# A pool of their own for the norms' small tiles, and a gap that puts large tiles at multiples of 512 bytes

## The chip, the cores and the metric

The kernel runs on one core of a Trainium2 chip. The metric is the time of one execution on the device in microseconds (us). Five engines work side by side: TensorE (PE in the rows; its weight loads are PEld), VectorE (DVE), ScalarE (ACT), GpSimd (POOL) and SyncE (SP), which issues the DMAs.

## The reference, cut to what matters

Two transformer blocks over 256 tokens of width 1024, all in float32. Nearly all of the arithmetic is in matrix products of the normed tokens with large weights:

```python
def first_block(x, p, ...):
    h = rmsnorm(x, norm_mix_g)
    u_rwkv, u_attn, u_gate = split(h @ w_in)
    o_a, o_b = rwkv7_time_mix(u_rwkv, ...), diff_attention(u_attn, ...)
    x = x + (sig(g_a) * (o_a @ w_proj_a) + sig(g_b) * (o_b @ w_proj_b)) @ w_out
    x = x + square(relu(rmsnorm(x, norm_mlp_g) @ w_ff1)) @ w_ff2          # 1024 -> 4096 -> 1024
    x = x + (p @ w_ple) * sigmoid(rmsnorm(x, norm_ple_g) @ w_ple_gate)
    return rmsnorm(x, final_norm_g)

def second_block(x, ...):
    for layer in range(2):
        x = x + 0.5 * swiglu(rms_norm(x, norm_ffn1[layer]), gate, up, down)   # 1024 -> 2816 -> 1024
        x = x + mix(rms_norm(x, norm_mix[layer]) @ w_in, ...) @ w_out[layer]  # attention
        x = x + 0.5 * swiglu(rms_norm(x, norm_ffn2[layer]), gate, up, down)
    return x
```

## The kernel before, in words

**Products.** A float32 product is made of three float32r products: each operand is split into a rounded high part and the rest, and `mm3` (which calls `mm`, the matmul of L279, three times) adds high x high, high x low and low x high in one PSUM bank. The stationary operand of a matmul is a 128x128 block of the tokens (transposed), the moving operand a 128x512 block of a weight; a chunk of 256 weight columns, and the attention's values, make 128x256 moving blocks, and the first block's queries and keys 128x384. In the rows `b<-hi,hTh` is such a matmul: bank, moving tile, stationary tile.

**Weights.** `wunit` brings 128x1024 floats (512 KB) into one of 3 `raw` buffers by a DMA on SyncE, `split` makes `hi` on ScalarE (L365) and `lo` on VectorE (L366). There are 5 buffers of each, and 6 more after the first stage.

**Tokens.** `Normed` (one for each 128 tokens) multiplies by the gain, flips by four PE transposes at a time (L283) and splits into `hTh` and `hTl`; its sum of squares `ss` and what `rstd` and `rsqrt` make of it are tiles of one to two floats a row. In `mlp` the gate's and up's products use hTh and hTl as stationary; the activation `a` is flipped into `aTh` and `aTl`, which are stationary for `down`. The first stage has `hT1h` and `hT1l` instead of hTh and hTl.

**Order.** The order of PE's instructions is written out by hand (`Weave` decides where side work is put between the large products); the other engines' order comes from the program's. Neither looks at addresses.

**Where tiles lie.** Each pool takes a stretch of the rows of SBUF in the order in which the pools are opened, and in a pool the tags follow each other in the order of first use; a tile takes its row's bytes, rounded up to 32. So a small tile shifts all that lie behind it. In the program as built the rows begin, in bytes and modulo 512:

| tile | pool | begins at | modulo 512 |
|---|---|---|---|
| x, h | xp, act | 17536, 25728 | 128 |
| ss, ms, rsi_x, rsh_x, rsa_x (two of each) | act | 42112 to 42431 | - |
| hTh, hTl (two of each) | act | 42432 to 58815 | 448 |
| sy, msg, r2 and the other small tiles of the last norm | act | 58816 to 59455 | - |
| raw | raw | 59456 | 64 |
| hi, lo (all eleven of each) | hl, hlx | 71744 | 64 |
| hT1h, hT1l | mix | 112704 | 64 |
| aTh, aTl of four of the five `mlp`s | mlp, ph0, ph2, ph5 | e.g. 172096 | 64 |
| aTh, aTl of the `mlp` before the second attention (ph3) | ph3 | e.g. 179296 | 96 |

In the last row the tile `fbias` (8 floats) lies ahead: the constants of the second attention are brought during that mlp, and shift it by 32 bytes. A column block of a tile begins a multiple of 512 bytes behind the tile, so it has the tile's residue. The only exception are blocks of the 264 columns of one attention weight (48 matmuls).

Of the kernel before, what the change touches and what calls it, by code (L numbers as in the profile page):

```python
# [7 lines left out]
F32 = mybir.dt.float32  # L8
# [100 lines left out]
class Mark:  # L109


    def __init__(self):
        self.done, self.at, self.res = False, 0.0, None
# [105 lines left out]
class Ker:  # L219


    def __init__(self, ctx, tc, d):
        self.tc, self.nc, self.d = tc, tc.nc, d
        nc = self.nc
        ctx.enter_context(tc.manual_schedule(engines={mybir.EngineType.PE}))
        self.W = Weave()
        self.const = ctx.enter_context(tc.tile_pool(name="const", bufs=1))
        self.xp = ctx.enter_context(tc.tile_pool(name="xp", bufs=1))
        self.act = ctx.enter_context(tc.tile_pool(name="act", bufs=2))
        self.ps = ctx.enter_context(tc.tile_pool(name="ps", bufs=1, space=PSUM))  # L230
        self.banks = Slots(self.W, self.ps, "b", [128, 512], 8)
        self.quota, self.held = 2, 0
        self.x = [self.xp.tile([128, D], F32, name=f"x{t}") for t in range(2)]
        self.pre = None

    def make_ident(self):
        nc = self.nc
        self.ident = self.const.tile([128, 128], F32, name="ident")
        nc.sync.dma_start(out=self.ident, in_=self.cst("ident"))
        self.identb = self.bf_const(self.const, "identb")  # L240
# [139 lines left out]
    def rsqrt(self, pool, m, n, tag):  # L380

        nc = self.nc
        i = pool.tile([128, n], I32, name=f"rsi_{tag}", tag=f"rsi_{tag}")
        mh = pool.tile([128, n], F32, name=f"rsh_{tag}", tag=f"rsh_{tag}")
        a = pool.tile([128, n], F32, name=f"rsa_{tag}", tag=f"rsa_{tag}")
        nc.vector.tensor_scalar(out=i, in0=m.bitcast(I32), scalar1=1, scalar2=None, op0=ALU.arith_shift_right)
        nc.vector.tensor_scalar(out=mh, in0=m, scalar1=-0.5, scalar2=None, op0=ALU.mult)
        nc.vector.tensor_scalar(out=i, in0=i, scalar1=-1.0, scalar2=float(0x5F3759DF), op0=ALU.mult, op1=ALU.add)
        y = i.bitcast(F32)
        for _ in range(3):  # L390
            if n == 1:
                nc.vector.scalar_tensor_tensor(out=a, in0=y, scalar=mh, in1=y, op0=ALU.mult, op1=ALU.mult)
            else:
                nc.vector.tensor_tensor(out=a, in0=y, in1=y, op=ALU.mult)
                nc.vector.tensor_tensor(out=a, in0=a, in1=mh, op=ALU.mult)
            nc.vector.scalar_tensor_tensor(out=y, in0=a, scalar=1.5, in1=y, op0=ALU.add, op1=ALU.mult)
        return y
# [15 lines left out]
        self.nc.scalar.activation(out=self.junk, in_=x[:, c], func=AF.Square, scale=scale, accum_out=ss[:, s:s + 1])  # L413

    def rstd(self, ss, tag):
        m = self.act.tile([128, 1], F32, name="ms", tag=f"ms{tag}")
        self.nc.vector.tensor_scalar(out=m, in0=ss[:, 0:1], scalar1=ss[:, 1:2], scalar2=1e-6, op0=ALU.add, op1=ALU.add)
        return m, self.rsqrt(self.act, m, 1, tag)

    def flip4(self, src, hi, lo):  # L420

# [79 lines left out]
    def attn_consts(self, pool, layer):  # L501
        nc = self.nc
        A = self.A = {"causal": self.bf_const(pool, "causal")}
        if layer == 0:
            A["stick"] = self.bf_const(pool, "stick")
            A["nsuf"] = self.ctile(pool, "nsuf")
            A["nones"] = self.ctile(pool, "nones")
            gains = {2: ("g_q_b_2", "g_k_b_2"), 3: ("g_q_b_2", "g_k_b_2")}
        else:
            A["tril"] = self.ctile(pool, "tril")  # L510
            A["ones"] = self.ctile(pool, "ones")
            A["dmask"] = self.bf_const(pool, "dmask")
            A["dcnt"] = self.bf_const(pool, "dcnt")
            gains = {0: ("g_q_c_2", "g_k_c_2"), 1: ("g_q_c_2", "g_k_c_2"), 2: ("g_q_d_2", "g_k_d_2"), 3: ("g_q_d_2", "g_k_d_2")}
        made = {}
        for g, pair in gains.items():
            if pair not in made:
                r = pool.tile([128, 2, 64], F32, name="grow", tag=f"grow{len(made)}", bufs=1)
                for i, n in enumerate(pair):
                    nc.sync.dma_start(out=r[:, i], in_=self.d[n].to_broadcast([128, 64]))  # L520
                nc.vector.tensor_scalar(out=r[:, 0], in0=r[:, 0], scalar1=0.125, scalar2=None, op0=ALU.mult)
                made[pair] = r
        self.gain = {g: made[pair] for g, pair in gains.items()}
        if layer == 1:
            self.fbias = pool.tile([128, 8], F32, name="fbias", tag="fbias", bufs=1)
            nc.sync.dma_start(out=self.fbias, in_=self.d["b_f_2"].to_broadcast([128, 8]))
        r = self.gain[3]
        self.rope = []
        for t in range(2):
            st = pool.tile([128, 128], F32, name="stage", tag="stage", bufs=2)  # L530
            nc.sync.dma_start(out=st[:, 0:64], in_=self.cst("cos", t * 64, 64))
            nc.sync.dma_start(out=st[:, 64:128], in_=self.cst("sin", t * 64, 64))
            cos, sin = st[:, 0:64], st[:, 64:128]
            gc = pool.tile([128, 2, 64], F32, name="gc", tag=f"gc{t}", bufs=1)
            gs = pool.tile([128, 2, 64], F32, name="gs", tag=f"gs{t}", bufs=1)
            for i in range(2):
                nc.vector.tensor_tensor(out=gc[:, i], in0=r[:, i], in1=cos, op=ALU.mult)
                nc.vector.tensor_tensor(out=gs[:, i, 0:32], in0=r[:, i, 32:64], in1=sin[:, 0:32], op=ALU.mult)
                nc.vector.tensor_tensor(out=gs[:, i, 32:64], in0=r[:, i, 0:32], in1=sin[:, 32:64], op=ALU.mult)
            self.rope.append((gc, gs))  # L540
# [242 lines left out]
    def attn_layer(self, pool, hT, layer, after):  # L783
# [29 lines left out]
        def queries(g, i):  # L813
# [18 lines left out]
            if kind == "stick":  # L832
                a = lambda j: (lambda h, x, y: qkT[0][half(h), j + h // 2, x:y])
                s = W.spawn(self.stick_group(pool, ready, a(2), a(0), vms[g], dst))
                sides[i] = [s, s]
                return
# [60 lines left out]
class Normed:  # L897


    def __init__(self, K, t, g, dst=None):  # L900
        self.K, self.t, self.g = K, t, g
        self.dst = dst or [K.act.tile([128, 8, 128], F32R, name=n, tag=n) for n in ("hTh", "hTl")]
        self.h = K.act.tile([128, D], F32, name="h", tag="h", bufs=4)
        self.ss = K.act.tile([128, 2], F32, name="ss", tag="ssx")
        self.sides = []

    def half(self, s, lat=3.0):
        c = slice(s * 512, s * 512 + 512)
        self.K.nc.vector.tensor_tensor(out=self.h[:, c], in0=self.K.x[self.t][:, c], in1=self.g[:, c], op=ALU.mult)
        self.flip(s, lat)  # L910
        self.K.square(self.K.x[self.t], s, self.ss)
        if s:
            self.m, self.r = self.K.rstd(self.ss, "x")
# [826 lines left out]
class FinalNorm(Normed):  # L1740


    def __init__(self, K, pool, t, g3, g34):
        Normed.__init__(self, K, t, g34)
        self.g3, self.sy = g3, K.act.tile([128, 2], F32, name="sy", tag="sy")
        self.y = pool.tile([128, D], F32, name="y", tag="y", bufs=2)

    def half(self, s):
        K, nc, x, y = self.K, self.K.nc, self.K.x[self.t], self.y
        c = slice(s * 512, s * 512 + 512)  # L1750
        nc.vector.tensor_tensor(out=self.h[:, c], in0=x[:, c], in1=self.g[:, c], op=ALU.mult)
        nc.vector.tensor_tensor(out=y[:, c], in0=x[:, c], in1=self.g3[:, c], op=ALU.mult)
        self.flip(s, 5.0)
        K.square(x, s, self.ss)
        K.square(y, s, self.sy)
        if s == 0:
            return
        _, r = K.rstd(self.ss, "f")
        m = K.act.tile([128, 1], F32, name="msg", tag="msg")
        r2 = K.act.tile([128, 1], F32, name="r2", tag="r2")  # L1760
        nc.vector.tensor_scalar(out=m, in0=self.sy[:, 0:1], scalar1=self.sy[:, 1:2], scalar2=None, op0=ALU.add)
        nc.vector.tensor_tensor(out=r2, in0=r, in1=r, op=ALU.mult)
        nc.vector.tensor_scalar(out=m, in0=m, scalar1=r2, scalar2=1e-6, op0=ALU.mult, op1=ALU.add)
        self.r = K.rsqrt(K.act, m, 1, "g")
        nc.vector.tensor_tensor(out=self.r, in0=self.r, in1=r, op=ALU.mult)
        nc.vector.tensor_scalar(out=x, in0=y, scalar1=r, scalar2=None, op0=ALU.mult)

# [86 lines left out]
```

## Time and profile before

| | |
|---|---|
| time, median of 3 runs | 1529.46 us (1527.96 to 1530.95) |
| the profiled execution | 1529.78 us, of which the span from the first to the last instruction is 1528.0 |
| mean granted clock of TensorE | 0.994 of full speed |
| PE busy | 1489.4 us, 97% |
| PEld, DVE, ACT, POOL busy | 81%, 61%, 50%, 3% |
| DMA | 51% of the 16 engines' time, 254.97 MB |

A busy share says that something runs, not at what rate: matmuls overlap each other in the profile, each is shown some 0.39 us long while the next starts after 0.23. The rate is read from the starts, or from the length of a stretch divided by its matmuls.

### The profile page before, as it was taken

How to read it: one execution, taken by the hardware profiler on the slowest of the kernel's cores; microseconds unless marked ns; L12 is line 12 of the kernel's file. 1: busy time of each engine (PE TensorE's matmuls, PEld its weight loads, DVE VectorE, ACT ScalarE, POOL GpSimd, SP SyncE). 2: the span in 40 equal slices, each digit the busy share in tenths (PEclk: the TensorE clock that was granted, in tenths of full speed). 3: DMA queues.
4: the chain of work that ended last, by engine and by line, in shares of the span. 5: the costliest groups of instructions: out<-in, count | busy, mean ns of one | idle time of the engine just before them, and what ended most of it. 6: DMA issues, size and time to landing. Idle time of an engine off the chain costs nothing.

```text
span 1528.0 us, 22440 instructions
## 1 busy us (share of the span) xinstructions
PE 1489.4 (97%) x8804; PEld 1237.2 (81%) x8804; DVE 927.9 (61%) x1528; ACT 760.8 (50%) x1142; POOL 46.7 (3%) x70
## 2 busy tenths in 40 slices
PE   7999989999999999999999999999999999999999
PEld 6887767788888788887888888887888888888887
DVE  5886777755558755557546554566545787565552
ACT  6644445644536544447565444445444566464441
POOL 1120100000000000001100000000000010000000
PEclk9999999999999999999999999999999999999999
DMA  7233238655544765536434665547555444275551
GB/s 253 90 118 107 98 119 278 202 194 177 182 151 157 223 200 190 185 132 193 138 111 147 198 194 192 179 156 220 190 189 182 141 154 136 78 227 180 179 182 53
DMA packets 76298, 254.97 MB, mean 167 GB/s; under 512 B 11040, under 2 KB 13344, under 8 KB 76192
## 3 DMA queue, kind: packets, MB, share of 16 engines
q1 hardware_dynamic: 76192, 253.53, 51.1%
q8 instruction: 69, 1.13, 0.3%
q14 instruction: 37, 0.30, 0.1%
HBM read 252.45 MB, written 1.05 MB: 166 GB/s over the span
## 4 chain that ended last, share of the span: by engine, by line
PE 81%; DVE 7%; DMA 5%; ACT 4%; issue 2%; POOL 0%; SPq 0%; ACTq 0%; DVEq 0%; POOLq 0%
PE b L279 77%; DMA raw<-in_w_dram 4%; PE b L283 4%; DVE lo L366 2%; ACT hi L365 2%; DMA grow<-in_norm_mix_g_dram 0%; DMA stage<-in_consts_dram 0%; DMA lam<-in_lam_k_dram 0%; POOL rb L563 0%; POOL rb L562 0%; DVE hTl L366 0%; DVE c L1132 0%; DVE U L1260 0%; DVE u L1129 0%; ACT e L376 0%
## 5 line engine op out<-in xcount | busy, mean ns | idle before, releaser
L366 DVE TENSOR_TENSOR lo<-raw,hi 128x1024 fp32r<-128x1024 f32 (+1 forms) x465 | 561.9, 1214 | 356.1 <-ACT hi L365 350.1
L365 ACT ACTIVATE hi<-raw 128x1024 fp32r<-128x1024 f32 (+1 forms) x465 | 485.6, 1050 | 417.4 <-PE b L279 207.6
L279 PE MATMUL b<-hi,hTh 128*128 128x512 f32 (+2 forms) x1312 | 499.9, 381 | 0.7 <-ACT hi L365 0.7
L279 PE MATMUL b<-hi,hTl 128*128 128x512 f32 (+2 forms) x1312 | 489.9, 373 | 0.5 <-DVE hTl L366 0.5
L279 PE MATMUL b<-lo,hTh 128*128 128x512 f32 (+2 forms) x1312 | 489.7, 373 | 0.8 <-DVE lo L366 0.8
L279 PEld LDWEIGHTS b<-hi,hTl 128*128 128x128 f32 x1312 | 247.4, 189 | 47.8 <-DVE hTl L366 0.9
L279 PEld LDWEIGHTS b<-hi,hTh 128*128 128x128 f32 x1312 | 247.6, 189 | 46.1 <-issue 2.5
L279 PEld LDWEIGHTS b<-lo,hTh 128*128 128x128 f32 x1312 | 247.8, 189 | 44.2 <-DVE lo L366 1.5
L279 PE MATMUL b<-hi,aTh 128*128 128x512 f32 x480 | 191.6, 399 | 0.0
L279 PE MATMUL b<-hi,aTl 128*128 128x512 f32 x480 | 188.1, 392 | 0.0
L279 PE MATMUL b<-lo,aTh 128*128 128x512 f32 x480 | 187.4, 390 | 0.0
L279 PEld LDWEIGHTS b<-hi,aTl 128*128 128x128 f32 x480 | 90.1, 188 | 20.1
L279 PEld LDWEIGHTS b<-lo,aTh 128*128 128x128 f32 x480 | 90.3, 188 | 18.0
L279 PEld LDWEIGHTS b<-hi,aTh 128*128 128x128 f32 x480 | 90.2, 188 | 17.6
L463 ACT ACTIVATE a<-b,rsi_x 128x512 f32<-128x512 f32 (+1 forms) x52 | 34.4, 662 | 55.3 <-PE b L279 55.2
L365 ACT ACTIVATE aTh<-b 128x512 fp32r<-128x512 f32 (+1 forms) x64 | 36.3, 567 | 43.2 <-PE b L283 41.8
L465 DVE SCALAR_TENSOR_TENSOR a<-b,rsi_x,a 128x512 f32<-128x512 f32 (+1 forms) x52 | 37.2, 716 | 32.1 <-PE b L279 17.3
L366 DVE TENSOR_TENSOR aTl<-b,aTh 128x512 fp32r<-128x512 f32 (+1 forms) x64 | 41.8, 653 | 20.0 <-ACT aTh L365 19.7
L279 PE MATMUL b<-hi,hT1h 128*128 128x512 f32 (+1 forms) x128 | 53.4, 418 | 0.0
L279 PE MATMUL b<-lo,hT1h 128*128 128x512 f32 (+1 forms) x128 | 47.8, 373 | 0.6 <-DVE lo L366 0.6
L279 PE MATMUL b<-hi,hT1l 128*128 128x512 f32 (+1 forms) x128 | 47.4, 371 | 0.0
L365 ACT ACTIVATE hTh<-b 128x512 fp32r<-128x512 f32 (+1 forms) x48 | 25.2, 541 | 38.1 <-PE b L283 33.5
(582 smaller groups left out, 1293.6 us busy)
## 6 DMA issues: line engine op xcount, KB each, us to landing
raw<-in_w_dram SPq DMA_DIRECT2D x446, 512.0 KB, 4.2
raw<-in_w_dram SPq DMA_DIRECT2D x16, 384.0 KB, 3.4
grow<-in_norm_ffn_dram SPq DMA_DIRECT2D x4, 512.0 KB, 5.3
x<-in_x_dram SPq DMA_DIRECT2D x4, 256.0 KB, 6.2
x<-in_x_dram SPq DMA_DIRECT2D x2, 512.0 KB, 4.4
grow<-in_norm_mix_dram SPq DMA_DIRECT2D x2, 512.0 KB, 4.8
out_dram<-x SPq DMA_DIRECT2D x4, 256.0 KB, 2.0
raw<-in_w_dram SPq DMA_DIRECT2D x2, 396.0 KB, 3.6
```

The source lines that it names most:

```text
L279: self.nc.tensor.matmul(out=out, lhsT=lhsT, rhs=rhs, start=start, stop=stop, skip_group_check=skip)
L283: self.nc.tensor.transpose(out=out, in_=src, identity=self.ident)
L365: self.nc.scalar.activation(out=hi, in_=src, func=AF.Copy)
L366: self.nc.vector.tensor_tensor(out=lo, in0=src, in1=hi.bitcast(F32), op=ALU.subtract)
L463: nc.scalar.activation(out=a[t], in_=p, func=AF.Silu if kind == "swiglu" else AF.Relu, scale=hT[t].r)
L465: nc.vector.scalar_tensor_tensor(out=a[t], in0=p, scalar=hT[t].r, in1=a[t], op0=ALU.mult, op1=ALU.mult)
```

## The change

The small tiles of the norms (`ss`, `sy`, and all that `rstd` and the last norm make) move from the pool `act` to a new pool `small`, opened before `xp`. A pool with one tile of 48 floats follows it (`line_up`; one memset of its first column on VectorE). `rsh` and `rsa` of the one-column `rsqrt` share one tag. `fbias` is made 128 floats wide, of which 8 are used.

```diff
         self.const = ctx.enter_context(tc.tile_pool(name="const", bufs=1))
+        self.small = ctx.enter_context(tc.tile_pool(name="small", bufs=2))
+        self.line_up(ctx, "a", 48)
         self.xp = ctx.enter_context(tc.tile_pool(name="xp", bufs=1))
...
+    def line_up(self, ctx, name, n):
+
+        if n:
+            pool = ctx.enter_context(self.tc.tile_pool(name=f"gap{name}", bufs=1))
+            self.nc.vector.memset(pool.tile([128, n], F32, name=f"gap{name}")[:, 0:1], 0.0)
...
-        mh = pool.tile([128, n], F32, name=f"rsh_{tag}", tag=f"rsh_{tag}")
-        a = pool.tile([128, n], F32, name=f"rsa_{tag}", tag=f"rsa_{tag}")
+        mh = pool.tile([128, n], F32, name=f"rsh_{tag}", tag=f"rsh_{tag if n > 1 else 'x'}")
+        a = pool.tile([128, n], F32, name=f"rsa_{tag}", tag=f"rsa_{tag if n > 1 else 'x'}")
...
-        m = self.act.tile([128, 1], F32, name="ms", tag=f"ms{tag}")
+        m = self.small.tile([128, 1], F32, name="ms", tag=f"ms{tag}")
...
-        return m, self.rsqrt(self.act, m, 1, tag)
+        return m, self.rsqrt(self.small, m, 1, tag)
...
-            self.fbias = pool.tile([128, 8], F32, name="fbias", tag="fbias", bufs=1)
+            self.fbias = pool.tile([128, 128], F32, name="fbias", tag="fbias", bufs=1)
+            self.fbias = self.fbias[:, 0:8]
...
-        self.ss = K.act.tile([128, 2], F32, name="ss", tag="ssx")
+        self.ss = K.small.tile([128, 2], F32, name="ss", tag="ssx")
...
-        self.g3, self.sy = g3, K.act.tile([128, 2], F32, name="sy", tag="sy")
+        self.g3, self.sy = g3, K.small.tile([128, 2], F32, name="sy", tag="sy")
```

The last norm's `msg`, `r2` and second `rsqrt` go to `small` in the same way. In the program as built, the small tiles then lie at 17536 to 18239, the gap at 18240, and x at 18432, h at 26624, hTh and hTl at 43008 to 59391, raw at 59392, hi and lo at 71680, and every aTh and aTl, hT1h and hT1l: all of them at 0 modulo 512. Most small tiles of the attention and of the first stage's recurrence keep residues of their own.

No engine's order changes but for the one memset. On VectorE the program began with these rows (`ln` and `P` are constants of the first stage, `h` the first tokens times the gain):

```order
1 L1090 MEMSET ln_346 128x1
2 L1197 MEMSET P 128x4 x2
3 L909 TENSOR_TENSOR h<-x_69,grow 128x512
4 L417 TENSOR_SCALAR ms<-ss 128x1
5 L909 TENSOR_TENSOR h<-x_69,grow 128x512
```

and begins now with these:

```order
1 L242 MEMSET gapa 128x1
2 L1099 MEMSET ln_354 128x1
3 L1206 MEMSET P 128x4 x2
4 L918 TENSOR_TENSOR h<-x_77,grow 128x512
5 L425 TENSOR_SCALAR ms<-ss 128x1
6 L918 TENSOR_TENSOR h<-x_77,grow 128x512
```

The memset of the gap stands ahead of all others; behind it the rows are the same, on this engine as on the others (line numbers apart).

## Rows read from the trace of the kernel before

**Rows 1.** The page: TensorE's busy time and clock, the chain that ended last.

```profile
PE 1489.4 (97%) x8804; PEld 1237.2 (81%) x8804; DVE 927.9 (61%) x1528; ACT 760.8 (50%) x1142; POOL 46.7 (3%) x70
...
PEclk9999999999999999999999999999999999999999
...
PE 81%; DVE 7%; DMA 5%; ACT 4%; issue 2%; POOL 0%; SPq 0%; ACTq 0%; DVEq 0%; POOLq 0%
PE b L279 77%; DMA raw<-in_w_dram 4%; PE b L283 4%; DVE lo L366 2%; ACT hi L365 2%; DMA grow<-in_norm_mix_g_dram 0%; DMA stage<-in_consts_dram 0%; DMA lam<-in_lam_k_dram 0%; POOL rb L563 0%; POOL rb L562 0%; DVE hTl L366 0%; DVE c L1132 0%; DVE U L1260 0%; DVE u L1129 0%; ACT e L376 0%
```

**Rows 2.** Groups of TensorE's instructions by tile and shape: xcount | busy us, mean ns.

```profile
L279 PE MATMUL b<-hi,hTh 128*128 128x512 f32 x1056 | 426.0, 403 | 0.7 <-ACT hi L365 0.7
...
L279 PE MATMUL b<-hi,aTh 128*128 128x512 f32 x480 | 191.6, 399 | 0.0
...
L279 PE MATMUL b<-hi,hTh 128*128 128x256 f32 x240 | 69.1, 288 | 0.0
```

**Rows 3.** The chain in order of time: start us, us, what; stretches without another engine.

```profile
676.20 5.49 PE b L279 x24
...
1183.89 5.59 PE b L279 x24
...
1189.91 5.59 PE b L279 x24
...
1362.71 16.80 PE b L279 x72
...
1505.82 18.43 PE b L279 x81
```

**Rows 4.** TensorE's groups from 1363 to 1379 us, then from 1506 to 1524.

```profile
L279 PE MATMUL b<-lo,hTh 128*128 128x512 f32 x24 | 9.5, 395 | 0.0
...
L279 PE MATMUL b<-lo,aTh 128*128 128x512 f32 x27 | 10.5, 389 | 0.0
```

**Rows 5.** Tile aTl from 1063 to 1200 us, then 1385 to 1510: ns min/median/max.

```profile
L279 PE MATMUL b<-hi,aTl x78: 389/395/400, 1063.6 to 1199.7; 128*128 128x512 f32 x78
L366 DVE TENSOR_TENSOR aTl<-b,aTh x9: 415/684/692, 1065.4 to 1185.7; 128x512 fp32r<-128x512 f32 x7, 128x256 fp32r<-128x256 f32 x2
...
L279 PE MATMUL b<-hi,aTl x63: 389/389/401, 1385.1 to 1509.6; 128*128 128x512 f32 x63
L366 DVE TENSOR_TENSOR aTl<-b,aTh x9: 415/691/693, 1386.6 to 1506.5; 128x512 fp32r<-128x512 f32 x7, 128x256 fp32r<-128x256 f32 x2
```

**Rows 6.** Timeline of TensorE: start us, us; 256 columns with 64 and 64.

```profile
25.29 0.28 PE L279 MATMUL b<-hT1h,hi 128*128 128x256 f32 x1
...
26.25 0.29 PE L279 MATMUL b<-hT1h,lo 128*128 128x256 f32 x1
```

**Rows 7.** The chain at 584 us, and TensorE's groups in that stretch.

```profile
584.49 19.76 PE b L279 x132
...
L279 PE MATMUL b<-lo,hTh 128*128 128x256 f32 x32 | 9.1, 284 | 0.0
...
L279 PE MATMUL b<-hi,aTh 128*128 128x512 f32 x12 | 4.8, 397 | 0.0
```

**Rows 8.** Timeline of TensorE where its clock was low, and that window.

```profile
202.46 0.63 PE L279 MATMUL b<-lo,hT1h 128*128 128x512 f32 x1
...
203.31 0.63 PE L279 MATMUL b<-hi,hT1h 128*128 128x512 f32 x1
...
202.00:206.00 4.00, 4.00 (x21) 3.12 (x21) 1.91 (x6) 0.00 (x0) 0.00 (x0) 0.75 0.20 79
```

**Rows 9.** The chain where weights came late, and TensorE's groups from 228.5 to 308.

```profile
242.47 4.71 DMA raw<-in_w_dram
...
L279 PE MATMUL b<-hi,hTh 128*128 128x512 f32 x96 | 38.7, 403 | 0.0
```

**Rows 10.** Timeline of VectorE at the start.

```profile
0.81 0.06 DVE L1090 MEMSET ln<- 128x1 f32 x1 [0.81 <-PEq L1842]
...
4.71 0.69 DVE L909 TENSOR_TENSOR h<-x,grow 128x512 f32<-128x512 f32 x1 [3.77 <-DMA grow<-in_norm_mix_g_dram]
```

More of the change, by code (lines that the diff above doesn't have):

```diff
@@ L1758, in half @@
         _, r = K.rstd(self.ss, "f")
-        m = K.act.tile([128, 1], F32, name="msg", tag="msg")
-        r2 = K.act.tile([128, 1], F32, name="r2", tag="r2")
+        m = K.small.tile([128, 1], F32, name="msg", tag="msg")
+        r2 = K.small.tile([128, 1], F32, name="r2", tag="r2")
         nc.vector.tensor_scalar(out=m, in0=self.sy[:, 0:1], scalar1=self.sy[:, 1:2], scalar2=None, op0=ALU.add)
@@ L1763, in half @@
         nc.vector.tensor_scalar(out=m, in0=m, scalar1=r2, scalar2=1e-6, op0=ALU.mult, op1=ALU.add)
-        self.r = K.rsqrt(K.act, m, 1, "g")
+        self.r = K.rsqrt(K.small, m, 1, "g")
         nc.vector.tensor_tensor(out=self.r, in0=self.r, in1=r, op=ALU.mult)
```

## The prediction

> **What bounds the kernel now.** I read the page first. TensorE is busy 97% of the span at the full granted clock, and the chain of work that ended last runs 81% over TensorE, 77% over the one matmul line [rows 1]. So the time is made where matmuls follow each other without a wait, and the question is at what rate they do. The busy share can't say, since each matmul is shown longer than the distance to the next one. I therefore took the chain in order of time, whose stretches are pure matmul, and divided each stretch by its count [rows 3]; the groups by tile say which operands a stretch has [rows 4].
>
> Two stretches of the same shape (128x512 moving, 128x128 stationary, no wait inside) run at different rates: 16.80 us for 72 with hTh and hTl as stationary, 233.3 ns each, and 18.43 us for 81 with aTh and aTl, 227.5 ns each [rows 3, 4]. The moving operand is the same kind of tile, hi or lo, at 64 modulo 512, in both. What differs is where the stationary tile begins: 448 for hT, 64 for aT.
>
> That it is the place and not the tile is shown by the fourth mlp, whose aT lies at 96. Its last product for 24 matmuls takes 5.59 us, twice, 232.9 each, where the same piece of the same code with aT at 64 takes 5.49, 228.8 each [rows 3]. The durations say it too: the median of the matmuls of aTl is 395 ns with 96 and 389 with 64, the minimum 389 in both [rows 5]. So in this trace stationary blocks at 64, the moving tile's own residue, go fast, and at 448 or 96 slow. (228.8 and 227.5 are both aT at 64: behind each set of four flips some matmuls run uneven, and 24 in a row have more of these than 81.)
>
> **The change, part by part.** *The memset.* One more on VectorE, 0.06 us by its neighbour, ahead of a 3.77 us wait for the gain's DMA [rows 10]. That wait hides it; without such cover it would cost its 0.06. The shared tags of `rsh` and `rsa` put writes behind reads on the same in-order engine, which costs nothing.
>
> *hTh and hTl go from 448 to 0.* The moving tiles go from 64 to 0 too, so stationary and moving begin at the same residue, as aT and hi do now. No row has the pair 0 and 0; the nearest row is the pair 64 and 64, which is equal as well: the change moves both by the same 64 bytes and keeps their relation. I take that price. 3 x 1056 = 3168 matmuls [rows 2] go from 233.3 to between 228.8 (pieces of 24) and 227.5 (81 in a row); the gain is 4.5 to 5.8 ns, and since hT's runs between flips are 24 to 72 long I take 5.0: 15.8 us (14.3 to 18.4).
>
> *aT of the fourth mlp goes from 96 to 0.* Of 3 x 480 matmuls [rows 2], (2816/128) x 2 x 2 x 3 = 264 are this mlp's. 232.9 to 228.8 makes 1.1 us.
>
> *Narrower products.* For 256 columns the pair 64 and 64 takes 0.96 us for 8 starts, 120.0 ns [rows 6]. The pair 64 and 448 is in the stretch of 132 at 584 us: 36 matmuls of 512 at 227.5 leave 11.57 us for 96 of 256 columns, 120.5 each [rows 7]. Equal, so nothing for these 720, nor for the 48 of 264.
>
> *The other engines.* VectorE's split into aTl takes 684 ns at 96 and 691 at 64 (median) [rows 5], no difference that an address makes; ScalarE and VectorE have slack anyway (50% and 61% [rows 1]). The weights' DMA now writes rows that begin at 0 instead of 64; it is 4% of the chain [rows 1], and no row prices the offset. The lower end is nothing; the upper is what a start 64 bytes off a row of 4096 can at most touch, 1.6% of those 61 us, 1.0 us. I take nothing, since the offset is small in a row, and keep the 1.0 us for the range.
>
> *What a faster TensorE runs into.* From 228.5 to 308 us the chain goes through weights that land late, 4.71 us from issue in one of the waits [rows 9]. There 3 x 96 matmuls of hT stand [rows 9], and their 288 x 5.0 = 1.4 us are given back, since the next weights arrive no sooner. Elsewhere the chain is on TensorE, and what becomes late next, the split of the next weight on VectorE, has 39% of idle time to move up in.
>
> *Sum:* 15.8 + 1.1 - 1.4 = 15.5 us off the profiled execution's 1529.8 us gives 1514.3; that execution lies 0.3 us above the median of the runs (1529.5), so I say 1514. With the ends of the terms, and up to 3 us given back at late weights, this case spans 1508 to 1519.
>
> **The rivals.** *A fixed cost goes as well.* Where the granted clock was low (0.75 over the window), 512 columns took 0.85 us for two starts, 425 ns, which is 512 columns at 1.2 GHz with nothing added [rows 8]. At 2.4 GHz they would be 213.3, and the best stretch has 227.5; 256 columns would be 106.7 and have 120.0 [rows 3, 6]. So every float32r matmul at the full clock carries some 13.3 ns, whatever its width. Every moving tile begins at 64 before, so the trace can't say whether the moving tile's place makes them. If it does, 6120 matmuls (3168 + 1440 of hT and aT at 512 columns, 216 of the first stage's and the early product's, 192 of 384, 1104 narrower) lose 13.3 ns, 81.4 us; on the path by TensorE's share of 81% [rows 1] 66 us, and the time is 1514 - 66 = 1448. If half of it goes: 1481. Against it: the addition is the same with the stationary tile at 448 and at 64 for 256 columns, and does not grow with the bytes moved, which fits a cost of changing the stationary block that stays. The Trainium skill, "TensorE: Matmul & The Clock Gate", section "Back-to-back issue gap", gives a warm gap of N/2.4 + 2.5 ns, 215.8 for 512 columns. By that figure 10.8 of the 13.3 ns would be avoidable; the sum would be about 1461 us, an estimate from that page. The trace before has no stretch near 215.8.
>
> *It becomes slower.* The pair 64 and 64 may be good because of 64, and 0 and 0 may be a pair at which both streams of reads meet, as 64 and 448 seem to. Then hT stays at 233 and the 1392 matmuls that are at 64 now (1176 of aT, 216 others) go from some 228.4 to 232.9: 1392 x 4.5 = 6.3 us, 1536 us. The point from which it decides: 4824 matmuls of 512 columns at x against 3168 x 233.3 + 264 x 232.9 + 1392 x 228.4, so x = 231.9 ns. Against it: two different residues are slow and the one equal pair is fast.
>
> *Nothing happens.* hT may be slow for another reason than its residue (its tiles lie between h and the weights, far from aT), and then only the 1.1 us of the fourth mlp come: 1528.7, which is within the 0.2% (3 us) that a measurement of this kernel can tell from no change. Against it: the fourth mlp. The Trainium skill, "SBUF — State Buffer", section "Specifications (TRN2)", speaks against the change too: it knows lines of 16 bytes in SBUF and asks for two hits in a line, and 0, 64, 96 and 448 all begin such a line. By that rule no matmul would change and the time would stay at 1529.5. The trace disagrees with it already: 5.59 against 5.49 us for the same 24 matmuls.
>
> **How the numbers follow.** The forecast (equal residues run as equal residues do now) has a chance of 0.57; part of the fixed cost goes, 1470 to 1505, 0.10; all of it goes, near 1450, 0.10; nothing, 0.10; slower, 0.13. Faster by over 0.2% is 0.77, within 0.2% 0.10, slower 0.13. The range reaches from the partial gain, 1475, to 1533, just above no change, and leaves out the whole of the fixed cost and most of the slower case, 2 in 10 together; the DMA's 1.0 us lies inside it. The likeliest case alone is 1508 to 1519.
>
> **What would show it.** Stretches of hT and aT at 228 to 229 ns for 512 columns, the same for the two, and the fourth mlp's pieces of 24 at about 5.49 us; 256 columns still at 120 ns; a count and order of instructions as before; VectorE's splits unchanged. I am wrong if 512 columns come near 214 to 222 ns (the moving tile's place cost something), or if aT's long stretch is above 227.5 (0 and 0 is not like 64 and 64), or if TensorE gains as forecast and the end doesn't move because the chain passes to the weights' DMA and split.

## The result, and the profile after

The changed kernel takes 1519.8 us (median of 4 runs, 1517.8 to 1521.1) against 1530.1 (1528.0 to 1531.0): a ratio of 0.9932, 95% interval 0.9917 to 0.9948, so 10.3 us faster where 15.5 were forecast. The profiled execution takes 1517.8 us. Its page, with the rows that answer to [rows 1]:

```profile
span 1516.0 us, 22441 instructions
...
PE 1473.4 (97%) x8804; PEld 1235.3 (81%) x8804; DVE 927.7 (61%) x1529; ACT 760.7 (50%) x1142; POOL 46.9 (3%) x70
...
PE 79%; DVE 7%; DMA 6%; ACT 5%; issue 2%; SPq 0%; POOL 0%; ACTq 0%; DVEq 0%; POOLq 0%
PE b L287 75%; DMA raw<-in_w_dram 5%; PE b L291 4%; DVE lo L374 3%; ACT hi L373 2%; DMA grow<-in_norm_mix_g_dram 0%; DMA stage<-in_consts_dram 0%; DMA lam<-in_lam_k_dram 0%; ACT L380 0%; DVE c L1141 0%; POOL rb L572 0%; DVE U L1269 0%; POOL rb L571 0%; DVE u L1138 0%; ACT e L384 0%
```

TensorE's busy time falls by 16.0 us, but the span by 12.0 (from 1528.0). The chain leaves TensorE by two points (81% to 79%), and the weights' DMA, the splits into `lo` and ScalarE gain what it loses. The instructions are the same but for the memset.

The chain in order of time (start us, us, what), at the places of [rows 3] and [rows 7]:

```profile
672.22 5.50 PE b L287 x24
...
1174.59 5.50 PE b L287 x24
1180.52 5.50 PE b L287 x24
...
1352.76 16.38 PE b L287 x72
...
1409.14 19.75 PE b L287 x132
...
1493.87 18.43 PE b L287 x81
```

hT's 72 matmuls take 16.38 instead of 16.80 us, now at 227.5 ns each, exactly the rate of aT's long stretch, which has not moved (18.43). The fourth mlp's pieces of 24 fell from 5.59 to the 5.50 of the others. The stretch of 132, 96 of them with 256 columns, stays (19.77 before). Over all pairs of successive starts that are under 245 ns apart, the mean distance for hT's 512 columns went from 232.6 to 227.9 ns, for the fourth mlp's aT from 233.0 to some 228.3; the other aT stay at 228.2 and 256 columns at 119.8 (119.3 before).

The tile aTl from 1062 us on (ns min/median/max), for [rows 5]:

```profile
L287 PE MATMUL b<-hi,aTl x74: 387/389/398, 1062.7 to 1194.1; 128*128 128x512 f32 x74
...
L374 DVE TENSOR_TENSOR aTl<-b,aTh x8: 418/684/692, 1085.0 to 1176.3; 128x512 fp32r<-128x512 f32 x6, 128x256 fp32r<-128x256 f32 x2
```

The matmuls' median is the fast one, and VectorE's split is what it was.

**Where four of TensorE's 16 us went.** The same matmul's start can be compared in both traces, since TensorE's order is unchanged. How much a stretch shortened, in us, beside what hT's matmuls in it would give at 4.6 ns each, and 4.8 for the 264 of the fourth mlp's aT. The last two columns are other pairs, told below (in apart128 the fourth mlp's aT is level already):

```
stretch in before   hT x512   at 4.6 ns   before-after   apart128-all64   light2 pair
   5 to  124            0       0.00          0.05          -0.82           1.34
 124 to  331          336       1.55          0.32           1.09          -0.63
 331 to  507 mlp      382       1.76          1.67           1.93           1.56
 507 to  553          146       0.67          0.27           2.94           0.45
 553 to  704 mlp      336       1.55          1.77           1.91           1.74
 704 to  802          168       0.77         -0.93          -0.52           0.10
 802 to  997 mlp      552       2.54          2.87           2.86           2.95
 997 to 1042          120       0.55          0.55           1.53           0.47
1042 to 1217 mlp      408       1.88 + 1.27   3.16           2.34           3.08
1217 to 1299          144       0.66         -0.72           0.27          -0.08
1299 to 1524 mlp      576       2.65          2.85           2.63           2.45
```

In the five long mlp stretches the gain is whole: 12.3 us seen for 11.7 worked out. The other five with hT hold 914 of its matmuls, worth 4.2 us, and come out 0.5 us longer. In some of them after's chain is not on TensorE. The chain by line between 508 and 552 us, first of before, then of after:

```profile
by line: PE b L279 83.6%; DMA stage<-in_consts_dram 9.6%; PE b L283 4.5%; DVE a L465 1.7%; DVE x L1766 1.5%; DVE gc L537 1.4%; DVE gs L539 0.9%; DVE rsa_g L392 0.9%; DVE gs L538 0.9%; DVE rsi_g L396 0.4%; issue 0.3%; DVE msg L1763 0.3%; DVE
```

```profile
by line: DMA raw<-in_w_dram 40.2%; DVE lo L374 14.7%; ACT hi L373 12.1%; PE b L287 9.3%; issue 8.5%; DVE a L473 3.3%; PE b L291 3.0%; DVE aTl L374 1.6%; DVE x L1775 1.5%; DVE gc L546 1.4%; DVE gs L548 0.9%; DVE rsa_g L400 0.9%; DVE gs L547 
```

In before TensorE bounded this stretch (84%), in after the weights' loads and splits do (67% together). The places alone do not explain that, because TensorE's granted clock fell here in before and not in after. Two windows of before, then of after; behind the engines' busy times stand the granted clock, the DMA share and GB/s:

```profile
500.00:525.00 25.00, 22.66 (x96) 18.02 (x95) 19.54 (x53) 14.05 (x18) 0.00 (x0) 0.93 0.67 209
690.00:715.00 25.00, 22.73 (x136) 19.16 (x135) 23.02 (x42) 18.47 (x33) 4.66 (x4) 1.00 0.74 231
```

```profile
500.00:525.00 25.00, 22.13 (x102) 18.00 (x102) 18.69 (x50) 13.83 (x17) 0.00 (x0) 1.00 0.67 204
690.00:715.00 25.00, 22.99 (x137) 19.11 (x136) 21.53 (x36) 15.71 (x31) 4.44 (x4) 0.93 0.65 213
```

The fall lies in these matmuls of before:

```profile
514.08 12.71 PE b L279 x48
```

They take 264.8 ns each instead of 232.6, 1.5 us more in all, which is more than the 0.7 us that hT's new place is worth in this stretch. The kernel all64, told below, has places equivalent to after's; its clock fell here too (0.93 from 500 to 525 us), and its chain by line stayed on TensorE:

```profile
by line: PE b L287 86.6%; PE b L291 5.5%; DVE a L473 1.7%; DVE x L1775 1.5%; DVE gs L548 0.9%; DVE gc L546 0.9%; DVE rsa_g L400 0.9%; DVE gs L547 0.9%; DVE rsi_g L404 0.4%; issue 0.3%; DVE msg L1772 0.3%; DVE rsi_g L396 0.2%; DVE rsi_g L394
```

So it is in every kernel that loads all its weights: TensorE bounds this stretch where its clock falls in it (before, all64, apart128, fbias8, raw5), and the weights do where it does not (after, apart64). What the new places alone did to it is not shown. At 704 us it is the other way round: the clock fell in after (0.93 from 690 to 715 us) and not in before, worth up to 1.7 us, as much as that stretch falls short of its 0.77. Without a fall there all64 takes 98.5 and fbias8 (also below) 97.9 us for the stretch of 704 to 802, and before 98.1, so hT's gain does not show there in any case. From 124 to 331 us the traces of before, after, all64, apart64, apart128 and fbias8 lie between 206.2 and 210.3 us, with no order by place, so 1.55 us can't be told there. There the loads follow each other in after at about the pace of [rows 9]:

```profile
236.37 5.17 DMA raw<-in_w_dram
```

TensorE's waits (engine, line, for whom: us in total, times, longest) show the other side. Two groups of before, then the same two of after:

```profile
PE b L283 <- DVE a L465: 2.7, 3, 2.3
...
PE b L283 <- DVE gate L1659: 1.8, 2, 1.0
```

```profile
PE b L291 <- DVE a L473: 4.8, 3, 2.9
PE b L291 <- DVE gate L1668: 3.8, 2, 2.2
```

4.1 us more of waiting, in flips at the mlp's change of stage (301, 509 and 546 us) and at the gates (250 and 258). Part of it differs from execution to execution: after and all64, whose places are equivalent, differ by 2.4 us from 124 to 331 and by 2.4 the other way ahead of it. The clock has a share in that: from 50 to 70 us it was 0.83 in after and 0.91 in all64, from 230 to 265 us 1.00 and 0.95.

### The profile page after: what moved, and what is told of

Same layout as the page of the kernel before. It is cut to its first block, busy times and chain, and to the rows that moved or that the text cites. A ratio compares the mean times of both kernels' runs of the same rounds, so it can differ in the third digit from the quotient of the medians.

```text
span 1516.0 us, 22441 instructions
## 1 busy us (share of the span) xinstructions
PE 1473.4 (97%) x8804; PEld 1235.3 (81%) x8804; DVE 927.7 (61%) x1529; ACT 760.7 (50%) x1142; POOL 46.9 (3%) x70
## 4 chain that ended last, share of the span: by engine, by line
PE 79%; DVE 7%; DMA 6%; ACT 5%; issue 2%; SPq 0%; POOL 0%; ACTq 0%; DVEq 0%; POOLq 0%
PE b L287 75%; DMA raw<-in_w_dram 5%; PE b L291 4%; DVE lo L374 3%; ACT hi L373 2%; DMA grow<-in_norm_mix_g_dram 0%; DMA stage<-in_consts_dram 0%; DMA lam<-in_lam_k_dram 0%; ACT L380 0%; DVE c L1141 0%; POOL rb L572 0%; DVE U L1269 0%; POOL rb L571 0%; DVE u L1138 0%; ACT e L384 0%
## 5 line engine op out<-in xcount | busy, mean ns | idle before, releaser
L287 PE MATMUL b<-lo,hTh 128*128 128x512 f32 (+2 forms) x1312 | 484.7, 369 | 0.8 <-DVE lo L374 0.8
L287 PE MATMUL b<-hi,hTl 128*128 128x512 f32 (+2 forms) x1312 | 484.9, 370 | 0.1
L374 DVE TENSOR_TENSOR hTl<-b,hTh 128x512 fp32r<-128x512 f32 (+1 forms) x48 | 29.2, 619 | 23.5 <-ACT hTh L373 23.5
```

The source lines that it names most:

```text
L287: self.nc.tensor.matmul(out=out, lhsT=lhsT, rhs=rhs, start=start, stop=stop, skip_group_check=skip)
L374: self.nc.vector.tensor_tensor(out=lo, in0=src, in1=hi.bitcast(F32), op=ALU.subtract)
```

## The experiments

**A table of residues.** The kernel is replaced by matmuls in the pattern of `mm3`, each pair of places 72 times:

```diff
...
+    for m in (0, 64):
+        for s in range(0, 512, 32):
+            for _ in range(3):
+                group(f"{s}_{m}", s // 4, m // 4, 512, s // 4)   # sh[:, s/4 + 128 k ...] against mh, ml[:, m/4 ...]
...
```

> The kernel is replaced by float32r matmuls alone (its output is not the reference's): for each pair of starting residues, 72 matmuls in a row in mm3's pattern (high, high, low stationary; high, low, high moving), stationary at s and moving at m modulo 512. Theory (the relation counts): every pair with s = m takes 16.3 us for 72 (226.7 ns each), whatever m is, and s different from m takes 16.6 to 16.8 (231 to 233). Rival A (the multiple of 512 counts): only s = m = 0 is fast, and 64 and 64 is not. Rival B (the fixed 13.3 ns hang on a start): some pair comes near 15.4 (214 each). The 256-column rows: 8.64 us for 72 (120 each) for all pairs.

The chain of that run; a name is the stationary tile's residue, the moving one's, and a running number (160 and 224 against 0, not shown, take 5.60 like 32):

```profile
150.48 5.44 PE 0_0_710 L1841 x24
...
166.97 5.60 PE 32_0_785 L1841 x24
...
183.76 5.60 PE 64_0_860 L1841 x24
...
200.57 5.62 PE 96_0_935 L1841 x24
...
217.40 5.57 PE 128_0_1010 L1841 x24
...
250.86 5.49 PE 192_0_1160 L1841 x24
...
284.08 5.44 PE 256_0_1310 L1841 x24
...
351.00 5.57 PE 384_0_1610 L1841 x24
...
384.46 5.49 PE 448_0_1760 L1841 x24
...
417.75 5.49 PE 0_64_1910 L1841 x24
...
450.98 5.44 PE 64_64_2060 L1841 x24
...
584.58 5.44 PE 320_64_2660 L1841 x24
...
651.50 5.57 PE 448_64_2960 L1841 x24
...
685.03 5.58 PE 4_0_3110 L1841 x24
...
795.23 8.64 PE 0_0_narrow L1841 x72
803.87 8.16 PE 448_0_narrow L1841 x72
```

For 512 columns the relation decides and the multiple of 512 does not: 64 and 64 is as fast as 0 and 0 (5.44 for 24, 226.7 ns). But the period is 256, not 512: 256 against 0 and 320 against 64 are just as fast. The place before the change, 448 against 64, takes 5.57, 232.1 ns, what the kernel had. And differing places are not all alike: 64 below the moving tile modulo 256 (192 or 448 against 0, 0 against 64) costs only 2 ns, 64 above costs 6.7. No pair comes below 226.7, so rival B falls. The last two rows are 256 columns: 120.0 ns level, but 113.3 with 64 below, so the expectation that all pairs are alike there was wrong.

**The kernel with everything at 64, hT moved apart, and fbias narrow.** Each edit by itself, on top of the changed kernel; the comments name the run:

```diff
-        self.line_up(ctx, "a", 48)
+        self.line_up(ctx, "a", 64)            # all64
...
+    K.line_up(ctx, "b", 16)                   # apart64, ahead of open_weights; 32 for apart128
...
-            self.fbias = pool.tile([128, 128], F32, name="fbias", tag="fbias", bufs=1)
+            self.fbias = pool.tile([128, 8], F32, name="fbias", tag="fbias", bufs=1)   # fbias8
```

> The gap is 64 floats instead of 48, so that every large tile begins at 64 modulo 512. Theory (the relation counts): the same as the changed kernel, 1519.8 us within 2, hT's stretches of 72 at 16.4 us. Rival (the multiple of 512 counts for the stationary tile): hT at 232.6 ns as before, 1530 us.

> The changed kernel with a second gap of 16 floats behind hT: hT stays at 0, the weights, hT1 and aT go to 64, the distance that hT had from the moving tiles before. Theory: hT's 3168 matmuls go back to 232.6 ns, 14.6 us more for TensorE; as TensorE's 16 us gained moved the end by only 10 to 12, the end should lose some 10 of them: 1528 to 1531 us. Rival (the pool of small tiles or the absolute place of hT made the gain): 1520 us.

> The changed kernel with fbias at 8 floats again: aT of the fourth mlp alone goes to 32 modulo 512. Theory: that mlp's last pieces of 24 take 5.58 us instead of 5.49, its 264 matmuls with aT cost 1.2 us more, about 1521 us. Rival (32 bytes are too near to matter): 5.49 us.

> The changed kernel with a second gap of 32 floats behind hT: hT at 0, the weights, hT1 and aT at 128, so that hT stands 384 above the moving tiles modulo 512, as it did before (448 against 64). Theory (distance modulo 256): hT's 3168 matmuls at 232.2 to 232.6 ns, stretches of 72 at 16.7 to 16.8 us, and 1529 us within 2. Rival (the pool of small tiles and the place at 0 made part of the gain): between 1520 and 1527.

| kernel | median us | ratio to before, 95% interval | hT's 512 columns |
|---|---|---|---|
| all64 | 1517.0 | 0.9907 (0.9883 to 0.9930) | 227.8 ns |
| apart64 | 1520.2 | 0.9928 (0.9906 to 0.9949) | 229.3 ns |
| apart128 | 1532.7 | 0.9997 (0.9985 to 1.0008) | 232.6 ns |
| fbias8 | 1515.2, one run | | 227.9 ns |

The stretch of 72 at some 1350 us in the chains of all64, apart128 and apart64, and fbias8's fourth mlp:

```profile
1350.12 16.35 PE b L287 x72
```

```profile
1365.17 16.80 PE b L287 x72
```

```profile
1355.24 16.48 PE b L287 x72
```

```profile
1166.24 5.59 PE b L287 x24
```

Beside all64, apart64 and fbias8 the kernel before took 1530.4 us, beside apart128 1533.9; the ratios are what compares. all64 is as fast as the changed kernel, the two intervals overlap. apart128 has the small pool, the gap, the wide fbias and hT at 0, and only the distance that hT had before: its stretch of 72 takes 16.80 us to the digit, and its time is that of before to within 0.2%. So the distance makes the gain of hT. apart64's expectation rested on a slip: 448 against 64 is 384 above, and 16 floats made it 448 above, which the table shows to be a cheap distance; the run agrees (229.3 ns). fbias8's pieces take 5.59 as expected. One run's time can't show the 1.2 us, since equivalent kernels lie between 1515 and 1521, but its trace does: from 1042 to 1217 us, where neither clock fell, it takes 173.1 us and after 171.9.

**Other widths.** The same table for narrower moving blocks, moving at 0:

> Matmuls alone again, now 24 in a row three times for other widths of the moving block, moving at 0 and stationary at s (width_s_0; its output is not the reference's). Theory from the table of 512 columns (a rate, 226.7/512 = 0.443 ns a column, that some distances reach): at the best distance 256 columns take 113.3 ns (2.72 us for 24), 384 take 170 (4.08), 264 take 116.9 (2.81), 128 take 56.7 (1.36). Rival (a fixed 13.3 ns for each matmul, as the prediction had it): 384 never under 173.3 (4.16), 264 never under 123.3 (2.96), 128 never under 66.7 (1.60). Which distance is best may differ by width: 256 columns were better 64 below the moving tile than level with it.

```profile
148.37 2.88 PE 256_0_0_710 L1841 x24
...
165.47 2.83 PE 256_64_0_860 L1841 x24
...
173.94 2.82 PE 256_96_0_935 L1841 x24
...
199.59 2.83 PE 256_192_0_1160 L1841 x24
...
217.89 4.16 PE 384_0_0_1310 L1841 x24
...
267.99 4.22 PE 384_128_0_1610 L1841 x24
...
317.24 2.88 PE 264_0_0_1910 L1841 x24
...
386.85 2.68 PE 128_0_0_2510 L1841 x24
...
513.61 5.44 PE 512_252_0_3185 L1841 x24
```

Neither theory holds for all. 384 columns stay at 173.3 ns or above, 160 + 13.3, as a fixed addition wants; a rate would have given 170. But 256 columns reach 117.5 here and 113.3 in the first table, less than the 120 of a fixed addition; 264 take 120.0, where it wants 123.3; and 128 columns take 111.7 at the three distances tried (0, 64 and 192).

**Weight work cut.** Two pairs of kernels, with the places of before and of after, load and split half of each weight block and use it twice. The first pair left blocks of 1024 columns whole; the second halves them too, by a few lines more that are not shown:

```diff
+            h = (k1 - k0 + 1) // 2
-            hi, lo = self.wunit(self.wsrc[u0 + k0 // per, :, :(k1 - k0) * n])
-            out += [(hi[:, i * n:(i + 1) * n], lo[:, i * n:(i + 1) * n]) for i in range(k1 - k0)]
+            hi, lo = self.wunit(self.wsrc[u0 + k0 // per, :, :h * n])
+            out += [(hi[:, i % h * n:(i % h + 1) * n], lo[:, i % h * n:(i % h + 1) * n]) for i in range(k1 - k0)]
```

> The kernel before, but of every weight block of two or more steps only the first half is loaded and split, and the second half of the steps uses it again: TensorE's matmuls, their order and their tiles' places stay, the DMA and split work falls (its output is not the reference's). Measured against the next run. Theory (TensorE's gain is given back at late weights): faster than before by several us, since the late weights of 228 to 308 us, 505 to 545 and 690 to 700 come in half the time; some 1500 to 1520. Rival (no wait on weights is on the path): 1530.

> The same cut in the changed kernel. Theory: it is faster than the cut kernel before by what TensorE gains, 14.5 to 16.5 us, not by the 10 to 12 of the full kernels. Rival (the rest is lost elsewhere, in the attention's chains): 10 to 12 us faster.

> The kernel before with the load and the split of every weight block halved, those of 1024 columns too, which the earlier cut left whole and at which that kernel still waited (213 to 241 us): TensorE's matmuls, their order and places stay (its output is not the reference's). Measured against the next run. Theory (what TensorE gains is swallowed where weights are late): the waits of 210 to 300 us go, about 1490 us. Rival: as the earlier cut, 1506.

> The same cut in the changed kernel. Theory: of the 914 matmuls of hT outside the large mlps' stretches (4.2 us) some 600 now run unhindered and 312 stand in the attention's chains, so this kernel is 14 to 15 us faster than the cut kernel before. Rival (they don't come through without late weights either): 11 to 12 us, the large mlps alone.

The first pair took 1506.0 and 1497.0 us (9.0 apart), the second 1499.7 and 1486.6 (13.0). Both kernels with the places of before are faster by 1.7% and 2.0%, so waits on weights are on the path, though the second misses its 1490. As to the differences, the first pair lies below theory and rival, the second between them. The table of stretches and the clock tell why neither settles it. In the first pair the clock fell at 498 us in light_after (0.97 from 500 to 525 us) and not in light_before (1.00), and light_after comes out 2.8 us longer from 507 to 553. Of the second pair's difference 1.3 us come from the first 124 us, where no hT stands. At the two short edges of mlps (507 to 553 and 997 to 1042) 0.9 of 1.2 us comes through with early weights, where before and after had 0.8; in the attention (704 to 802, 1217 to 1299) nothing of 1.4. From 124 to 331 us it stays open: light2_after's clock fell there (0.95 from 230 to 265 us, 1.00 in light2_before), worth 1.7 us where 1.55 are at stake, and even the halved loads still end the chain there:

```profile
214.20 5.76 DMA raw<-in_w_dram
```

**More raw buffers.** Two more of `raw` behind the first stage, for one fewer of hi and lo, on top of the changed kernel:

```diff
+        self.rawx = ctx.enter_context(self.tc.tile_pool(name="rawx", bufs=2))   # in more_weights
...
+        if len(self.hls) > 1 and self.turn * 3 // 5 == (self.turn - 1) * 3 // 5:
+            rp = self.rawx                                                      # in wunit, else rawp
...
-    K.more_weights(ctx, 6)
+    K.more_weights(ctx, 5)
```

> The changed kernel with two more raw buffers behind the first stage, and one fewer of hi and lo for them (hlx 5 instead of 6); all residues stay at 0. Theory (late weights swallow part of the gain): more loads under way at the change of stage, the stretch of 228 to 308 us gets 2 to 6 us shorter, 1512 to 1518 us. Rival (the DMA's rate is the limit there, or the hi and lo buffers are): no change from 1517 to 1520, or slower for the missing hi and lo.

It takes 1509.7 us, ratio 0.9861 (0.9837 to 0.9884), an interval below that of the changed kernel: a version that beats both, and by 2 us more than its range allowed. The two profiled executions are 5.8 us apart (raw5's is the slowest of its four runs, after's the fastest). Against the trace of after, 1.9 us come from 997 to 1042, where after's chain leaves TensorE for a late unit and raw5's does not. First after, then raw5:

```profile
1020.16 10.95 PE b L287 x48
...
1031.69 1.07 ACT hi L373
...
1032.78 1.24 DVE lo L374
```

```profile
1015.93 10.94 PE b L287 x48
...
1027.30 16.37 PE b L287 x72
```

2.7 us come from 124 to 331, 0.7 from 507 to 553. Another 2.6 come from the first 124 us, which the edit doesn't touch; some 1.6 of them are the clock's, which from 50 to 70 us was 0.91 in raw5 and 0.83 in after. 1.0 is lost from 331 to 507.

**Narrow blocks 64 above hT.** raw5, and blocks of 256 columns begin 16 floats into `hi` and `lo`, three blocks to a unit instead of four:

```diff
...
+def narrow(key, n):
+    return n == 256 and key[0] != "w_in"
...
+        hi = pool.tile([128, self.unit], F32R, tag="hi", name="hi")[:, o:]   # o = 16 for a narrow block, lo too
...
```

> The kernel with five raw buffers, and the blocks of 256 weight columns of the second block packed three to a unit instead of four, which leaves room to let them begin 64 bytes into hi and lo: hT then stands 64 below them modulo 256, the distance at which 256 columns took 113.3 ns alone and 117.7 in the kernel with everything at 64. Theory: 720 matmuls go from 119.8 ns to between 113.3 and 117.7, 1.5 to 4.7 us less for TensorE, of which the 384 in the mlps reach the end: 0.8 to 2.5 us, 1507 to 1509 us, if the 16 units more cost nothing. Rival (the units cost more than the distance gives): 1510 or more.

1510.4 us, ratio 0.9854 (0.9828 to 0.9879): no different from raw5. The 117.7 of the expectation is a number of apart64, where hT is at 0 and the weights at 64; with everything at 64 it is 119.7. The 256-column matmuls went from 119.8 to 117.8 ns, at the slow end of what was expected, 1.4 us in all, and the runs (1507.1 to 1514.5) scatter more than that.

## Why the prediction was right, and what was mis-sized

The likeliest case came true in its mechanism: hT and aT now run at one rate, and the kernel is faster by over 0.2%. Its size did not quite: 1519.8 us lies in the stated range, but above the 1508 to 1519 of this case alone. Point by point:

- **hT, 3168 matmuls by 5.0 ns, 15.8 us.** The mechanism is right and shown by apart128 and the table. The size is 4.6 to 4.7 ns, 14.6 to 14.9 us: the 233.3 came from a stretch of 72, and all of hT's unhindered starts have a mean of 232.6.
- **aT of the fourth mlp, 1.1 us.** 233.0 to some 228.3 for 264, 1.2 to 1.3 us; fbias8 undoes it (5.59 for 24).
- **Equal residues modulo 512.** Right where it was applied, but the period is 256 for 512 columns (the table). The "slower" rival, that 64 and 64 is good because of 64, falls with 0 and 0 at the same 5.44 alone and all64 in the kernel.
- **The fixed 13.3 ns.** They did not go: 512 columns stay at 226.7 at best. The Trainium skill, "TensorE: Matmul & The Clock Gate", section "Back-to-back issue gap", gives N/2.4 + 2.5 ns as the gap of a matmul by itself at the full clock, 215.8 ns for 512 columns. No pair of the table comes near it.
- **"Nothing happens."** Falls with 12 us in the trace. The Trainium skill, "SBUF — State Buffer", section "Specifications (TRN2)", names lines of 16 bytes. The table is not explained by them, for stationary tiles at 32, 64, 96 and 128 all begin such a line, and take 5.57 to 5.62 us against a moving tile at 0, instead of 5.44.
- **256 columns, the memset, VectorE's splits, nothing.** As forecast: 19.75 against 19.77 for the stretch of 132, 684 ns for the split, and the memset takes 0.06 us ahead of a wait of 3.65 us for the gain's DMA in the trace of after.
- **1.4 us given back at late weights.** This is the term that was mis-sized, and the step behind it was "elsewhere the chain is on TensorE". 914 matmuls stand in stretches where the chain leaves TensorE, not 288, and their 4.2 us did not show: those stretches together came out 0.5 us longer. In the attention VectorE, ScalarE and GpSimd share the chain, and at 509 us it passed to the weights' loads in after, where the clock did not fall. 14.6 + 1.3 - 4.2 = 11.7 is near what the profiled pair shows (12.0), but the clocks of the two traces differ stretch by stretch by as much as the terms, so the agreement is in part luck; the medians' 10.3 differ from it by no more than the interval allows.

What swallowed the 4.2 us is not shown in full. In the attention nothing comes through even with early weights (the second pair) and without a fall of the clock (all64, fbias8), which points to the attention's own chains. At 997 to 1042 nothing was lost (0.55 of 0.55): raw5 shows that weights are late there, not that they took hT's gain. At 507 to 553 the clock of before and the loads of after can't be told apart, and for 124 to 331 it stays open.

## What to carry to other kernels

Put the stationary and the moving tiles of a dense float32r stretch of 512 columns at the same residue modulo 256, and look for small tiles that shift one of them: here it cost one memset of 0.06 us, and 2% of these matmuls' rate hangs on it. Find the effect by dividing a wait-free stretch by its count, and compare stretches of one shape, since busy shares and means over shapes hide it. When the bound engine gets faster, count the gain only in stretches where another engine has room, and look for the next bound (here the raw buffers) in the others. Before a stretch's difference is put down to the change, compare its granted clock in both traces.

## What the runs showed of the hardware

- 512 columns of float32r take 226.7 ns when both tiles begin at the same residue modulo 256 and 228.7 to 234.2 at the other multiples of 32 tried. 4 bytes below is as fast as level (5.44 for 24), 4 bytes above is not (5.58).
- The distance is not symmetric: 64 below the moving tile costs 2 ns, 64 above 6.7. For 256 columns the order turns round: level takes 120.0, 64 below 113.3 in one run and 117.9 in the other. The first was 448 against 0, the second 192 against 0, so for 256 columns the period may be 512; the kernels with hT at 0 and the weights at 64 take 117.8, and the cause stays open.
- 128 columns with a new stationary block each take 111.7 ns, hardly less than the best of 256 columns. That fits a least distance between two matmuls with new stationary blocks; no run tested it.
- TensorE's granted clock is not the same in every execution of one kernel: beside all64, before's runs went from 1527.1 us at a mean clock of 0.997 to 1537.1 at 0.992. Nor does it fall at the same places in kernels with the same order of work: from 500 to 525 us it was 0.93 in before, with a wait of TensorE of 2.3 us just ahead, and 1.00 in after, with one of 2.9.
